# Streaming encoder layer on Trainium2: the last phase in blocks of 768, 768 and 576 tokens, with the sample in the last block and seven-product pairs in all three

## The chip, the cores and the metric

One NeuronCore of a Trainium2 chip runs the whole layer. The metric is device microseconds of one execution: the median of three runs before the change is 2979.64 us (2978.55 to 2980.76). TensorE is called PE in the profile (its weight loads PEld), VectorE DVE, ScalarE ACT, GpSimd POOL, SyncE SP.

## The reference

One encoder layer works on a prompt of 2048 tokens and on a sample of 64 tokens with caches of its own. Both have model width 1024; the FFN has 2816 columns. In short, for each of the two:

```
h = rms_norm(x) * (1 + sc1) + sh1
z = h @ w_in                      # conv pair, q, k, v, two gates
conv_out = conv_module(...)       # depthwise conv, layer norm, swish, projection
attn_out = band_attend(...) @ w_attn_out
merged = sigmoid(g_conv) * conv_out + sigmoid(g_attn) * attn_out
x = x + gt1 * (merged @ w_o)
h2 = rms_norm(x) * (1 + sc2) + sh2
gate, up = split(h2 @ w_ffn_in)
x = x + gt2 * ((silu(gate) * up) @ w_ffn_out)
```

The shifts, scales and gates (`sh`, `sc`, `gt`) differ between prompt and sample. All is float32.

## The kernel before

**Products.** TensorE multiplies float32 as a sum of two shorter numbers, high and low. Each product is three matmuls, high by high, high by low and low by high (`mm3`). Both operands must first be split: ScalarE copies the high half, VectorE or GpSimd subtracts it from the whole and writes the low half. For weights these are the tiles `whi` and `wlo`. For the 64 sample tokens the high and low halves lie side by side in 128 columns, so that two matmuls do (`mm2`); the two halves of the result are added later.

**Phases.** Up to about 1199 us the projections, the convolution, the attention and the gates run, in four blocks of tokens (`PBLOCKS`), and leave their results in DRAM. From there on the last phase runs (the loop over `CBLOCKS`, line 1823). It takes blocks of tokens, (0, 576), (576, 1344), (1344, 2112), where tokens 0 to 63 are the sample. The change touches this phase only. A block goes through these steps:

- *Merge* (`merge`, line 1690): in two chunks of tokens, the attention projection and the gating of the two branches. The gates come in by DMA a channel tile at a time (`gate_columns`), the branches' values by `load_mixed`. The chunks of the block of 576 are 320 and 256 tokens, those of a block of 768 are 384 and 384.
- *Output projection* (`wo`, line 1857): for each tile of 128 tokens, 1024 columns in two banks `pw`. The first `shared` of the eight steps of the sum are taken for all tiles of the chunk together, the others tile by tile.
- *Residual* (`residual`, line 1729, a generator for each tile): gate, add `x`, norm, transposes by TensorE (`pw<-ident,xn`), scale and shift, and the operands of the first FFN product, `b11`, `b21`, `b22` and the sums `t1` to `t4`, which are sums over the four quarters of the transposed block (first and second half of the tokens by first and second half of the 1024 columns). VectorE and ScalarE make them, 512 elements at a time.
- *Early half products* (line 2216 on): the first FFN product of a row goes by seven products instead of eight. Those with `b11` and `b21` need only the first half of the tokens, and for the first `EARLY` = 5 rows they are taken while the operands of the second half are still being made. Their results wait in `early`.
- *FFN rows*: 22 rows `f` of 128 gate and 128 up columns. `up` (line 1961) takes the products of a row, each 12 matmuls of `half` columns (288 or 384), with VectorE and ScalarE adding between them; `hidden` and `rest` write the result of a row, split, into `hid`.
- *Second FFN product*, for a pair of rows at a time, between the products of the next rows. The direct way (`down`, `add_down`) takes 12 matmuls of 512 columns for a tile and row pair (8 for the sample), and VectorE adds each tile's two halves into `acc`. The other way (`down_pair`, line 2053) takes seven products instead of eight for a pair of rows, two halves of the tokens and two halves of the columns. It needs sums of `hid` (tile `sums`, made in `rest`) and sums of weights, which GpSimd makes in `sum_second`, and each product is added by VectorE on its own. `seven(s, f)` (line 564) says which rows of which block go by it: rows 4 to 19 of the second and third block, none of the first.
- *End of a block*: the last two rows (four in the first block) are added, scaled and written out. In the last block GpSimd scales `acc` and adds `x1` ahead of the last matmuls (`scale`, `add_last`).

**Weights.** The class `Weights` (line 264) loads slabs in the order of `weight_order`, splits them ahead of their use (`split`, line 451) and keeps the split ones in a small ring. Sums of first-product weights (`s1` to `s4`) are made by GpSimd in the first block and stored to DRAM (`sum_d`), from where the later blocks read them. In `split` the low half of a slab goes to GpSimd as a rule; for `up` and `fo` slabs it goes to VectorE where GpSimd, by the planner's count, is more than 3000 ns behind TensorE:

```
late = key[0] in ("up", "fo") and self.stream.load["pool"] - self.stream.load["pe"] > POOL_BEHIND
e, name = (self.dve, "dve") if on_dve or late else (self.gps, "pool")
```

**Order.** The program is written as generators with due times (`stream`, `turns`, `work`), which keep a running count of what each engine has been given. A scheduler then puts the instructions of each engine in a fixed order, and each engine works through its own in that order. Every operation passes through one helper, so that the profile shows line 102 for nearly all of them; they are told apart by the names of their tiles (`pw` output projection, `ps` merge and first FFN product, `pd` second FFN product).

## Time and profile before

| what | us |
|---|---|
| median of the runs (lowest, highest) | 2979.64 (2978.55, 2980.76) |
| the profiled execution, its span | 2979.5, 2977.7 |
| first block of the last phase, from the first merge matmul to the last scaled sum | 1199.2 to 1715.2 |
| second block | 1715.2 to 2343.7 |
| third block, up to its last matmuls | 2343.7 to 2971.0 |
| last additions and the output | 2971.0 to 2977.7 |

The profile is of one execution. A line of the timeline gives start, length, engine, source line, operation, output and input tiles, shape, count, and in square brackets the idle time of the engine before it and what released it. In a group of instructions the columns are the shape and count, then busy time and the mean of one in ns, then the idle time before them. The chain of waits is followed back from the last instruction: at each step to what released it, or to the instruction before it on its engine. The mean granted clock of TensorE is 0.995 of full speed.

### The profile page before, as it was taken

What the parts mean: (1) busy time and instruction counts of PE and PEld (TensorE: products, weight loads), DVE (VectorE), ACT (ScalarE), POOL (GpSimd) and SP (SyncE); (2) the same over time, 40 slices, a digit from 0 to 9 for tenths busy, and PEclk for the clock granted to TensorE, in tenths of its full rate; (3) what the DMA queues carried; (4) which work ended last, traced back from release to release, by engine and by line L of the source; (5) the groups of instructions that cost most, each with busy time, mean ns of one, the idle gap of its engine ahead of it and who ended that gap; (6) DMA issues with size and microseconds to landing.
All of it is one profiled execution on the core that took longest, in us unless ns stands there. A gap on an engine that the chain in (4) does not pass through costs nothing.

```text
span 2977.7 us, 44838 instructions
## 1 busy us (share of the span) xinstructions
PE 2900.2 (97%) x16199; PEld 2593.1 (87%) x16199; DVE 2025.9 (68%) x3637; ACT 1356.8 (46%) x2441; POOL 1127.7 (38%) x727
## 2 busy tenths in 40 slices
PE   7999899999999999989999999999999999999999
PEld 4899777787888888888999999999999999999998
DVE  5797677767856886577777755666666557466666
ACT  2345642662456257464444345534444345344442
POOL 0201310111011102454466443255666741465667
PEclk9999999999999999999999999999999999999999
DMA  8889889878987798885444786333333975333333
GB/s 290 300 286 310 270 279 312 284 251 274 306 283 224 267 263 278 262 288 175 145 145 159 244 263 235 116 95 106 114 113 113 316 239 184 93 95 114 114 103 128
DMA packets 467723, 628.05 MB, mean 211 GB/s; under 512 B 36276, under 2 KB 314664, under 8 KB 467501
## 3 DMA queue, kind: packets, MB, share of 16 engines
q1 hardware_dynamic: 453456, 605.58, 62.8%
q10 hardware_dynamic: 14045, 19.60, 1.9%
q8 instruction: 127, 2.08, 0.3%
q14 instruction: 95, 0.78, 0.1%
HBM read 476.53 MB, written 148.54 MB: 210 GB/s over the span
## 4 chain that ended last, share of the span: by engine, by line
PE 82%; DVE 7%; DMA 4%; ACT 2%; issue 2%; POOL 2%; SPq 0%; ACTq 0%; POOLq 0%; DVEq 0%
PE ps L102 53%; PE pd L102 16%; PE pw L102 6%; DVE y L102 2%; PE sc L102 2%; PE po L102 2%; PE ptp L102 2%; DVE wlo L102 1%; PE pt L102 1%; DMA kk<-k_d 1%; ACT whi L102 1%; PE pa L102 1%; POOL r L102 1%; DVE pw L102 1%; DMA wst<-in_w_in 0%
## 5 line engine op out<-in xcount | busy, mean ns | idle before, releaser
L102 PE MATMUL ps<-t,whi 128*128 128x384 f32 (+1 forms) x2112 | 503.1, 322 | 8.7 <-ACT t L102 4.9
L102 POOL TENSOR_TENSOR wlo<-wst,whi 128x1024 fp32r<-128x1024 f32 (+1 forms) x156 | 356.4, 2294 | 279.0 <-ACT whi L102 262.6
L102 ACT ACTIVATE whi<-wst 128x1024 fp32r<-128x1024 f32 (+1 forms) x263 | 256.8, 979 | 331.2 <-PE ps L102 119.8
L102 PE MATMUL ps<-b,whi 128*128 128x384 f32 (+1 forms) x1584 | 381.7, 326 | 7.0 <-DVE early L102 3.6
L102 PEld LDWEIGHTS ps<-t,whi 128*128 128x128 f32 x2112 | 367.8, 188 | 16.3 <-ACT t L102 5.1
L102 DVE SCALAR_TENSOR_TENSOR y<-u,wd,y 128x512 f32<-128x512 f32 (+1 forms) x480 | 369.0, 773 | 6.3
L102 PE MATMUL ps<-hh,whi 128*128 128x512 f32 (+2 forms) x992 | 361.7, 365 | 0.0
L102 DVE TENSOR_TENSOR acc<-acc,pd 128x512 f32<-128x512 f32 x464 | 311.7, 685 | 62.7 <-PE pd L102 60.2
L102 PE MATMUL ps<-hl,whi 128*128 128x512 f32 (+2 forms) x992 | 345.6, 348 | 0.0
L102 PE MATMUL ps<-hh,wlo 128*128 128x512 f32 (+2 forms) x992 | 345.4, 348 | 0.0
L102 PE MATMUL ps<-t,wlo 128*128 128x384 f32 (+1 forms) x1056 | 339.4, 322 | 0.8 <-POOL wlo L102 0.7
L102 PE MATMUL pd<-whi,hid 128*128 128x512 f32 x972 | 314.8, 390 | 0.0
L102 PEld LDWEIGHTS ps<-b,whi 128*128 128x128 f32 x1584 | 278.7, 189 | 13.1 <-DVE early L102 4.5
L102 POOL TENSOR_TENSOR r<-t,mhalf 128x1 f32<-128x1 f32 (+3 forms) x68 | 83.6, 1232 | 462.1 <-DVE t L102 457.0
L102 PE MATMUL ps<-b,wlo 128*128 128x384 f32 (+1 forms) x792 | 257.3, 325 | 0.0
L102 ACT ACTIVATE pr<-pr,sm 128x640 f32<-128x640 f32 (+3 forms) x272 | 200.1, 747 | 112.1 <-DVE sm L102 109.5
L102 PEld LDWEIGHTS pd<-whi,hid 128*128 128x128 f32 x972 | 182.5, 188 | 37.7 <-ACT hid L102 0.7
L102 PEld LDWEIGHTS ps<-hh,wlo 128*128 128x128 f32 x992 | 186.7, 188 | 21.6
L102 PEld LDWEIGHTS ps<-hh,whi 128*128 128x128 f32 x992 | 187.2, 189 | 18.5 <-issue 1.6
L102 PEld LDWEIGHTS ps<-hl,whi 128*128 128x128 f32 x992 | 187.5, 189 | 15.5 <-issue 1.4
L102 PEld LDWEIGHTS ps<-t,wlo 128*128 128x128 f32 x1056 | 198.2, 188 | 2.2 <-POOL wlo L102 1.3
L102 PE MATMUL pd<-wlo,hid 128*128 128x512 f32 x508 | 198.6, 391 | 0.0
(226 smaller groups left out, 6170.6 us busy)
## 6 DMA issues: line engine op xcount, KB each, us to landing
whi<-w_din_h SPq DMA_DIRECT2D x72, 512.0 KB, 6.5
wlo<-w_din_l SPq DMA_DIRECT2D x72, 512.0 KB, 8.4
wst<-sum_d SPq DMA_DIRECT2D x132, 256.0 KB, 2.7
wfo<-in_w_ffn_out SPq DMA_DIRECT2D x64, 512.0 KB, 3.2
wmod<-in_w_ada SPq DMA_DIRECT2D x46, 512.0 KB, 6.5
sum_d<-ws SPq DMA_DIRECT2D x88, 256.0 KB, 2.8
wst<-in_w_ffn_in SPq DMA_DIRECT2D x84, 256.0 KB, 3.1
wst<-in_w_in SPq DMA_DIRECT2D x40, 512.0 KB, 8.8
```

What stands on the lines that cost most here:

```text
L102: self.last = f(*args, **kw)
```

## The change

The blocks of the last phase become the tokens (64, 832), (832, 1600) and (1600, 2112), and the sample (tokens 0 to 63) joins the last one (`MIXED` = 2). It lies in the middle there: two prompt tiles, the sample, two prompt tiles, so that each half of the tokens is 256 prompt tokens and 32 of the sample. The merges of that block have chunks of 320 (256 and the sample) and 256 tokens. In code:

- `block_tiles`, `block_chunks` and `width` take the place of `tile_chunks`; a chunk is a list of parts, so that `gate_columns` and `load_mixed` issue one DMA for each part.
- `seven`: in the first block the pairs f // 2 = 2, 4, 6, 8 go by seven products, in the two others all rows from 2 to 19.
- In the last block `down_pair` has two tiles in each product (`wide` = 256) and takes the sample directly with `mm2`, for which the last weight slab of a pair holds `b12` beside `b22` (`down_operands`). `hid` keeps the sample's high and low halves behind the prompt tokens (`both`), written by `hidden_sample`.
- In `rest` the split of the sum kept in `sums[2]` moves from the even row of a pair to the odd one, and the tile `sums` is taken only there.
- `scale` and `add_last` treat the sample's tile in the last block: its two halves are added with a ScalarE copy between two VectorE additions.
- `shared` is 6 of 8 steps wherever a chunk has two tiles.

```diff
...
 PBLOCKS = [(0, 576), (576, 1088), (1088, 1600), (1600, 2112)]
-CBLOCKS = [(0, 576), (576, 1344), (1344, 2112)]
+CBLOCKS = [(64, 832), (832, 1600), (1600, 2112)]
+MIXED = 2
 STEP_NS = 500.0
...
-def tile_chunks(lo, hi):
-    tiles = token_tiles(lo, hi)
-    t, n = tiles[(len(tiles) + 1) // 2 - 1]
-    return [(lo, t + n), (t + n, hi)]
+def block_tiles(s):
+    tiles = [(t, P, t - CBLOCKS[s][0]) for t in range(*CBLOCKS[s], P)]
+    if s == MIXED:
+        tiles = tiles[:2] + [(0, SMP, 2 * P)] + [(t, n, a + SMP) for t, n, a in tiles[2:]]
+    return tiles
+def block_chunks(s):
+    lo, hi = CBLOCKS[s]
+    n = (hi - lo) // 2
+    return [[(0, lo, n)] + [(n, 0, SMP)] * (s == MIXED), [(0, lo + n, n)]]
+def width(parts):
+    return sum(n for _, _, n in parts)
...
-        return {"b11": (0,), "t1": (0,), "t3": (0, 1)}.get(op, (1,))
+        return {"b11": (0,), "b12": (0,), "t1": (0,), "t3": (0, 1)}.get(op, (1,))
...
-    return s > 0 and 4 <= f < NF - 2
+    return 2 <= f < NF - 2 if s else f // 2 in (2, 4, 6, 8)
...
-DOWN_OPERANDS = (("b11", "b21"), ("t3", "t2"), ("t1", "t4"), ("b22",))
+def down_operands(s):
+    return ("b11", "b21"), ("t3", "t2"), ("t1", "t4"), ("b22", "b12") if s == MIXED else ("b22",)
...
                 if f >= 2 and seven(s, f - 2):
-                    yield from (("dn", s, f - 2, *DOWN_OPERANDS[i]) for i in {0: (0,), 2: (1, 2), 4: (3,)}.get(j, ()))
+                    yield from (("dn", s, f - 2, *down_operands(s)[i]) for i in {0: (0,), 2: (1, 2), 4: (3,)}.get(j, ()))
                 elif j == 0 and f >= 2 and f - 2 not in last_rows(s):
...
-            shared = KT - 2 if not s and c1 == hi else 4
+            shared = KT - 2 if len(grp) < 3 else 4
...
+        side = half - 2 * P if s == MIXED else 0
+        wide = half - side
+        inner = [slice(0, wide), slice(side, half)]
+        rows_at = [slice(i * wide, (i + 1) * wide) for i in range(2)]
+        both = slice(2 * wide, 2 * wide + 2 * SMP)
+        at_rows = {t: slice(a - (a > half) * (half - wide + side), a - (a > half) * (half - wide + side) + n) for t, n, a in tiles}
         def hidden(f, i, ps):
             h = hid_of(f)
-            c = slice(i * half, (i + 1) * half)
             stream.after("act", "dve")
-            if s:
-                split(h[:, 0, c], h[:, 1, c], ps)
+            split(h[:, 0, rows_at[i]], h[:, 1, rows_at[i]], ps[:, inner[i]])
+            hidden_sample(f, i, ps)
+        def hidden_sample(f, i, ps):
+            if s != MIXED:
                 return
-            hi = h[:, 0, SMP:][:, c]
-            act.activation(hi, ps, AF.Copy)
-            stream.after("dve", "act")
-            cut = 0 if i else SMP
-            if cut:
-                dve.tensor_tensor(h[:, 0, :cut], ps[:, :cut], hi[:, :cut].bitcast(F32), ALU.subtract)
-            dve.tensor_tensor(h[:, 1, c][:, cut:], ps[:, cut:], hi[:, cut:].bitcast(F32), ALU.subtract)
+            c = slice(0, side) if i else slice(wide, half)
+            hi, lo = (hid_of(f)[:, 0, both.start + l * SMP + i * side :][:, :side] for l in range(2))
+            stream.after("act", "dve")
+            split(hi, lo, ps[:, c])
...
                 return
-            if "t" not in sums:
-                sums["t"] = wk.tile([P, 4, 2, CW // 2], F32R, tag="m1", name="sums")
-            at = lambda i: [sums["t"][:, i, l, :half] for l in range(2)]
+            at = lambda i: [sums["t"][:, i, l, :wide] for l in range(2)]
+            z, whole, y = z[:, inner[0]], y, y[:, inner[1]]
             if f % 2 == 0:
+                hidden_sample(f, 1, whole)
                 sums["a21"], sums["s3"] = (
-                    wk.tile([P, CW // 2], F32, tag=name, name=name, bufs=1)[:, :half] for name in ("a21", "s3")
+                    wk.tile([P, CW // 2], F32, tag=name, name=name, bufs=1)[:, :wide] for name in ("a21", "s3")
                 )
...
                 stream.after("act", "dve")
-                split(*at(2), y)
                 act.activation(sums["s3"], y, AF.Copy)
                 return
-            hidden(f, 1, y)
-            t = bank("gp")
+            if "t" not in sums:
+                sums["t"] = wk.tile([P, 4, 2, CW // 2], F32R, tag="m1", name="sums")
+            hidden(f, 1, whole)
+            split(*at(2), sums["s3"])
+            t = bank("gp")[:, :wide]
             dve.tensor_tensor(t, y, sums["a21"], ALU.add)
...
-            a11, a12, a22 = (
-                [hid[0][:, e, l, i * half : (i + 1) * half] for l in range(2)] for e, i in ((0, 0), (1, 0), (1, 1))
-            )
-            s1, s2, s3, s4 = ([sums["t"][:, i, l, :half] for l in range(2)] for i in range(4))
-            n = len(tiles) // 2
+            a11, a12, a22 = ([hid[0][:, e, l, rows_at[i]] for l in range(2)] for e, i in ((0, 0), (1, 0), (1, 1)))
+            s1, s2, s3, s4 = ([sums["t"][:, i, l, :wide] for l in range(2)] for i in range(4))
+            n = wide // P
             zs = [bank_of("gp", "pd")]
...
                     stream.after("dve", "pe")
-                    dst = acc[p + i * n][:, 512 * e : 512 * e + 512]
+                    dst = acc[p + i * (len(tiles) - n)][:, 512 * e : 512 * e + 512]
                     dve.tensor_tensor(dst, dst, pss[p], ALU.add)
-            w = W.get(("dn", s, f, *DOWN_OPERANDS[0]))
+            def sample(ps, w, es, j):
+                for e, (h, l) in zip(es, ((t[0][:, i], t[1][:, i]) for t, i in w)):
+                    mm2(ps, hid[0][:, e, 0, both], h, l, e == es[0], e == es[1])
+                stream.after("dve", "pe")
+                dst = acc[n][:, 512 * j : 512 * j + 512]
+                dve.tensor_tensor(dst, dst, ps, ALU.add)
+            ops = down_operands(s)
+            w = W.get(("dn", s, f, *ops[0]))
             products(ys, a11, w, 0, True, False, 0, 0)
             yield
-            zs += [bank_of(tag, "pd") for tag in ("y1", "z1")]
+            zs += [bank_of(tag, "pd") for tag in ("y1", "z1")[: n - 1]]
             products(zs, a12, w, 1, True, True, 0, 0)
+            if s == MIXED:
+                sample(bank_of("gp", "pd"), ((w, 0), (w, 1)), (0, 1), 0)
             W.done()
-            w = W.get(("dn", s, f, *DOWN_OPERANDS[1]))
+            w = W.get(("dn", s, f, *ops[1]))
             products(zs, s3, w, 0, True, False, 1, 1)
...
             W.done()
-            w = W.get(("dn", s, f, *DOWN_OPERANDS[2]))
+            w = W.get(("dn", s, f, *ops[2]))
             products(ys, s1, w, 0, False, False, 1, 1)
...
             yield
-            w = W.get(("dn", s, f, *DOWN_OPERANDS[3]))
+            w = W.get(("dn", s, f, *ops[3]))
             products(ys, s4, w, 0, False, True, 0, 1)
+            if s == MIXED:
+                sample(bank_of("z1", "pd"), ((w, 0), (w, 1)), (1, 0), 1)
             W.done()
...
         def pieces():
-            return [(i, t, n, j) for i, (t, n) in enumerate(tiles) for j in range(2)]
+            return [(i, t, n, j) for i, (t, n, _) in enumerate(tiles) for j in range(2)]
...
-            gt = [wk.tile([P, 512], F32, tag="ws", name="gt", bufs=4) for _ in range(2)]
-            for j in range(2):
-                nc.sync.dma_start(gt[j], gt_d[1, 0:1, 512 * j : 512 * j + 512].to_broadcast([P, 512]))
-            ends["gt"] = gt
+            gt = ends["gt"] = {}
+            for which in {int(t < SMP) for t, _, _ in tiles}:
+                gt[which] = [wk.tile([P, 512], F32, tag="ws", name="gt", bufs=4) for _ in range(2)]
+                for j in range(2):
+                    nc.sync.dma_start(
+                        gt[which][j], gt_d[1, which : which + 1, 512 * j : 512 * j + 512].to_broadcast([P, 512])
+                    )
             yield stream.load["pe"] + DMA_LAG
             for k, (i, t, n, j) in enumerate(pieces()):
-                dst = acc[i][:n, 512 * j : 512 * j + 512]
-                gps.tensor_tensor(dst, dst, gt[j][:n], ALU.mult)
+                dst = acc[i][:, 512 * j : 512 * j + 512]
+                gps.tensor_tensor(dst, dst, gt[int(t < SMP)][j], ALU.mult)
                 ends["scaled"] = k
...
             for k, (i, t, n, j) in enumerate(pieces()):
-                ps = bank_of("gp", "pd")[:n]
-                c, f = slice(t - lo, t - lo + n), slice(512 * j, 512 * j + 512)
+                ps = bank_of("gp", "pd")
+                c, f = at_rows[t], slice(512 * j, 512 * j + 512)
                 for e, w in zip(last, ws):
                     h = hid_of(e)
-                    mm3(ps, h[:, 0, c], h[:, 1, c], w[0][:, 0, f], w[1][:, 0, f], e == last[0], e == last[-1])
+                    at = w[0][:, 0, f], w[1][:, 0, f], e == last[0], e == last[-1]
+                    if t < SMP:
+                        mm2(ps, h[:, 0, both], *at)
+                    else:
+                        mm3(ps, h[:, 0, c], h[:, 1, c], *at)
                 while ends.get("scaled" if after(k) else "added", -1) < k:
...
                 stream.after("dve", "pe")
-                dve.tensor_tensor(ps, ps, ends["gt"][j][:n], ALU.mult)
+                dve.tensor_tensor(ps, ps, ends["gt"][int(t < SMP)][j], ALU.mult)
                 dst = acc[i][:n, f]
+                if t < SMP:
+                    dve.tensor_tensor(ps, ps, acc[i][:, f], ALU.add)
+                    stream.after("act", "dve")
+                    act.activation(dst, ps[SMP : 2 * SMP], AF.Copy)
+                    stream.after("dve", "act")
+                    ps = ps[:n]
                 dve.tensor_tensor(dst, dst, ps, ALU.add)
...
```

## What the change does to the time: a prediction

> **What bounds the kernel now.** I read the page first, the busy times of each stage next, and then the chain of waits, the waits of TensorE and the timelines of the stages that the change touches.
>
> ```profile
> span 2977.7 us, 44838 instructions
> PE 2900.2 (97%) x16199; PEld 2593.1 (87%) x16199; DVE 2025.9 (68%) x3637; ACT 1356.8 (46%) x2441; POOL 1127.7 (38%) x727
> ```
>
> The profiled execution took 2979.5 us (span 2977.7), the runs have a median of 2979.64, so a sum made against the profiled one needs no correction beyond 0.1 us. TensorE is busy 97% of the span: work taken from it counts in full, and all else counts only where it makes TensorE wait. The stretches of the three blocks, the end, one stretch of direct rows in the block of 576 and one of pairs with seven products in a block of 768 follow; the columns are the stretch, its length, and busy us (instructions) of PE, PEld, DVE, ACT and POOL, then clock, DMA share, GB/s.
>
> ```profile
> 1199.20:1715.15 515.95, 501.55 (x3113) 461.56 (x3114) 364.89 (x622) 230.65 (x441) 268.32 (x169) 0.99 0.63 204
> 1715.15:2343.65 628.50, 627.16 (x3290) 584.27 (x3289) 388.96 (x645) 279.35 (x458) 348.44 (x203) 1.00 0.47 151
> 2343.65:2971.00 627.35, 625.92 (x3283) 583.02 (x3283) 386.36 (x642) 273.98 (x453) 345.20 (x205) 1.00 0.45 147
> ...
> 1484.00:1660.00 176.00, 175.22 (x1119) 162.85 (x1118) 126.99 (x195) 72.80 (x150) 116.98 (x75) 1.00 0.46 149
> 2000.00:2306.00 306.00, 306.00 (x1613) 287.51 (x1612) 198.78 (x328) 137.66 (x238) 200.58 (x122) 1.00 0.36 113
> ```
>
> The two blocks of 768 leave TensorE idle for 1.3 and 1.4 us each, the block of 576 for 14.4. So there are two places to gain: TensorE's work, and the gaps of the first block. Where the gaps lie, TensorE's waits from the last output-projection tile on say (us in all, times, longest): first the first block, then the second.
>
> ```profile
> PE ps L102 <- ACT t L102: 4.9, 1, 4.9
> PE ps L102 <- DVE early L102: 2.6, 1, 2.6
> PE ps L102 <- DVE u L102: 1.6, 1, 1.6
> PE ps L102 <- ACT early L102: 0.8, 2, 0.5
> ```
>
> ```profile
> PE ps L102 <- DVE early L102: 0.5, 1, 0.5
> PE ps L102 <- POOL wlo L102: 0.3, 1, 0.3
> PE ps L102 <- ACT early L102: 0.2, 1, 0.2
> ```
>
> That is 9.9 us against 1.0. The timeline of TensorE shows a second cost behind the long waits.
>
> ```profile
> 1306.69 0.39 PE L102 MATMUL pw<-whi,m 128*128 128x512 f32 x1
> ...
> 1318.72 0.73 PE L102 MATMUL ps<-b,whi 128*128 128x288 f32 x2 [2.63 <-DVE early L102]
> ...
> 1319.49 0.68 PE L102 MATMUL ps<-b,whi 128*128 128x288 f32 x2
> ...
> 1320.21 0.68 PE L102 MATMUL ps<-b,whi 128*128 128x288 f32 x2
> ...
> 1322.85 0.42 PE L102 MATMUL ps<-b,whi 128*128 128x288 f32 x2
> ...
> 1323.25 0.43 PE L102 MATMUL ps<-b,whi 128*128 128x288 f32 x2
> ...
> 1329.06 0.58 PE L102 MATMUL ps<-t,whi 128*128 128x288 f32 x1 [4.85 <-ACT t L102]
> ```
>
> A triplet of 288-wide matmuls takes 0.40 us (1322.85 to 1323.25), behind the wait 0.72 (1319.49 to 1320.21). Four triplets go so, 4 x 0.32 = 1.3 us, and the same follows the 4.85 us wait. The start of the first block thus costs 9.9 + 2 x 1.3 = 12.5 us, that of a block of 768 only 1.0.
>
> **1. Fewer matmuls.** The durations come from the chain of waits, one pair of rows of the 768 block and one of the 576 block (start, us, what).
>
> ```profile
> 2634.21 20.93 PE ps L102 x120
> ...
> 2665.58 6.16 PE pd L102 x27
> ...
> 1483.53 11.20 PE ps L102 x83
> 1494.73 12.71 PE pd L102 x56
> ```
>
> A `pd` matmul costs 6.16/27 = 0.228 us (12.71/56 = 0.227), a 384-wide one 20.93/120 = 0.174, a 288-wide one 11.20/83 = 0.135. The first FFN product keeps its matmuls, only the order of the three half widths becomes 384, 384, 288. The second loses some. A direct pair of rows takes 72 `pd` matmuls with 768 tokens, 56 with 576 (48 for four tiles, 8 for the sample); by seven products 63, and in the mixed last block 42 + 8 = 50.
>
> Before: 11 x 56 + 2 x (8 x 63 + 3 x 72) = 616 + 1440 = 2056. After: (4 x 63 + 7 x 72) + (9 x 63 + 2 x 72) + (9 x 50 + 2 x 56) = 756 + 711 + 562 = 2029. The order in which the instructions stand on TensorE has these 27 fewer too. 27 x 0.2276 = 6.1 us, in stages where TensorE is 99.6 to 100% busy: **-6.1**, sure.
>
> **2. Start of the first block.** It now has 3 + 3 tiles and 384 columns, so the ten half products of the five early rows (120 matmuls) cover 120 x 0.174 = 20.9 us in place of 120 x 0.135 = 16.2. These 4.7 us are about the wait for `t` (4.85): it goes with its 1.3 us of slow clock, and the 1.6 us for `u` behind it is worked off: -7.8. What stays is the wait for `early`: the operand sums of the early rows are still made by GpSimd here, and ScalarE and VectorE stand in order behind them.
>
> ```profile
> 1316.24 1.15 ACT L102 ACTIVATE whi<-ws 128x512 fp32r<-128x512 f32 x2 [2.32 <-POOL ws L102]
> ...
> 1316.90 1.08 DVE L102 TENSOR_TENSOR wlo<-ws,whi 128x512 fp32r<-128x512 f32 x1 [5.17 <-ACT whi L102]
> ```
>
> Bounds: it becomes like the second block's start, 1.0 - 12.5 = -11.5; or the third tile's work on VectorE uses up nearly all cover, -2. I take **-8**.
>
> **3. Start of the last block.** This is the reverse: 3 + 2 tiles (the sample the third) with 288 columns, where a 768 block stood. In its instruction order TensorE reaches the first product with `t3` after 72 half-product matmuls and 16 transposes, 72 x 0.135 + 16 x 0.13 = 11.8 us behind the last output-projection matmul (0.13 by the eight of 1.03 us below). `t3` needs the last tile's norm, transposes and sums. In the second block these took from 1850.90 to 1874.9, 24.0 us with three tiles:
>
> ```profile
> 1850.90 0.39 PE L102 MATMUL pw<-whi,m 128*128 128x512 f32 x1
> ...
> 1853.26 1.03 PE L102 MATMUL pw<-ident,xn 128*128 128x128 f32 x8
> ...
> 1874.24 0.68 DVE L102 TENSOR_TENSOR t<-pw,t 128x512 fp32r<-128x512 f32 x1
> ```
>
> One tile less is about nine 512-wide VectorE steps of 0.6 each (the last row, net of its overlap with the next), 5.4 us, so `t3` is there after 18.6: a wait of 6.8, then 1.3 of slow clock, about 1 more for the rows behind: **+9**. Queued behind the waiting matmul are the rest of the half products, though their data are there. Bounds: +4 if the order lets the cover decide (4.7 less cover, next to the 1.0 there), +12 if it goes as the first block did (12.5). The merges before it are 320 and 256 wide rather than 384 and need 16 + 4 + 2 more DMA issues on SP for the sample's gates, inputs and scales; SP only queues loads that have a whole merge of lead: +0.5 (0 to +3).
>
> **4. Pairs of the last block.** The rule that moves a slab's low half from GpSimd to VectorE fires far oftener there: by the order of the instructions 63 `up` slabs of 1024 in the last block against 15 before. Each pair now has on VectorE 7 slabs of 1024, 16 accumulations of 512, 14 operations of 288, 11 of 256, 4 of 32; GpSimd keeps 12 of 512. TensorE's pair takes 168 x 0.135 + 50 x 0.228 = 34.1 us.
>
> ```profile
> L102 DVE TENSOR_TENSOR acc<-acc,pd 128x512 f32<-128x512 f32 x50 | 33.0, 682 | 15.2 <-PE pd L102 15.1
> ...
> L102 DVE TENSOR_TENSOR wlo<-wfo,whi 128x1024 fp32r<-128x1024 f32 x5 | 8.8, 1767 | 2.4 <-ACT whi L102 2.4
> ...
> L102 DVE SCALAR_TENSOR_TENSOR s<-tg,ps 128x288 f32<-128x288 f32 x10 | 4.5, 449 | 3.0 <-ACT tg L102 3.0
> ...
> L102 DVE TENSOR_TENSOR hid<-ps,hid 128x64 fp32r<-128x64 f32 x10 | 2.2, 217 | 2.4 <-ACT hid L102 2.4
> ```
>
> ```profile
> 1869.92 1.22 DVE L102 TENSOR_TENSOR wlo<-wst,whi 128x1024 fp32r<-128x1024 f32 x1
> 1871.05 0.41 DVE L102 TENSOR_SCALAR pw<-pw,A,B 128x128 f32<-128x128 f32 x1
> ```
>
> Each operation overlaps the next by about 0.08 (1.22 against 1871.05 - 1869.92 = 1.13). Net of that: 16 x 0.60 + 7 x 1.14 + 14 x 0.37 + 11 x 0.33 + 4 x 0.14 = 9.6 + 8.0 + 5.2 + 3.6 + 0.6 = 27.0 us of 34.1, 79%; with 1767 ns a slab, as beside a busy GpSimd, 27.0 + 7 x 0.63 = 31.4, 92%. At 127/176 = 72% TensorE lost only 0.8 of 176 us. So VectorE is not full, but more of its in-order work stands ahead of the `hid` that TensorE needs. Cover: one row of first products. I take **+2** (0 to +14: two such slabs a pair, 1.26 us, in eleven pairs).
>
> **5. The rest.** Each of the four pairs by seven products in the first block adds nine accumulations on VectorE (21 for 12, 9 x 0.6 = 5.4 us) and the sums and splits of `hid`, beside GpSimd's operand sums; in the 768 blocks the same pairs cost TensorE nothing (306.00 busy of 306.00), and a direct pair stands between any two here: +1 (0 to +4). The split of a pair's second sum moves to its odd row, off the path. In the end the sample's piece waits for a ScalarE copy between VectorE additions; 66 matmuls hide it, except for the last pieces:
>
> ```profile
> 2955.83 15.18 PE pd L102 x66
> ...
> 2973.63 0.69 DVE L102 TENSOR_TENSOR acc<-acc,pd 128x512 f32<-128x512 f32 x1
> ```
>
> The last pieces belong to prompt tiles again: +0.3 (0 to +4).
>
> **Sum:** -6.1 - 8 + 9 + 0.5 + 2 + 1 + 0.3 = -1.3, so 2979.5 - 1.3 = 2978.
>
> **Rivals.** *A faster start, both times.* Block 0 starts like the second block (-11.5), the last block's start costs only its cover (+4), pairs cost nothing: -6.1 - 11.5 + 4 + 0.5 + 1 + 0.3 = -11.8, 2968. For it: the 1.0 us of the second block's start; against it: `t3` stands early in TensorE's order, and GpSimd's sums stay in block 0.
>
> *VectorE decides in the last block.* It begins when a slab takes 1.77 us rather than 1.14 and two of them a pair stand just ahead of a `hid` split: 11 x 1.26 = 13.9 in place of 2, -1.3 + 11.9 = +10.6, 2990. For it: 63 slabs instead of 15, the two rows below, and 72% being the highest load seen without loss; against it: GpSimd is busy there only 12 x 1.3 = 15.6 of 34.1 us, 46%, where the 1767 ns were measured at 117/176 = 66%.
>
> ```profile
> 1560.02 1.92 DVE L102 TENSOR_TENSOR wlo<-wst,whi 128x512 fp32r<-128x512 f32 x1 [0.16 <-ACT whi L102]
> ...
> 1567.63 0.69 DVE L102 TENSOR_TENSOR wlo<-ws,whi 128x512 fp32r<-128x512 f32 x1
> ```
>
> The same operation takes 1.92 us or 0.69. The Trainium skill, "SBUF — State Buffer", section "Who interferes with whom", says that a VectorE instruction with two SBUF inputs and a GpSimd instruction that reads SBUF exclude each other for a whole instruction; these rows agree with it, and it speaks against moving slabs to VectorE. By that rule alone each of the seven slabs could lose up to 1.23 us, 8.6 in a pair, which would fill VectorE (35.6 of 34.1).
>
> *It does not do what it says.* The counts on TensorE rule it out.
>
> **Numbers.** Forecast 0.42, own range 2970 to 2986 by the bounds of steps 2 to 4; faster rival 0.28; VectorE rival 0.30. About 0.2%, 6 us, is what a measurement of this kernel can tell from no change. Of the forecast 0.13 lies more than 6 us below, 0.22 within, 0.07 above; of the first rival 0.27 below; of the second 0.28 above, the rest within. So faster 0.40, same 0.25, slower 0.35. The range reaches past both rivals' values, 2964 to 2993.
>
> **What would show it.** 27 fewer `pd` matmuls at 0.228. Step 2: TensorE's waits from the first block's last output-projection matmul on fall from 9.9 to some 4. Step 3: one wait of some 7 us for `t` or `pw` at the last block's start. Step 4: TensorE's idle time in the last block's pairs stays under 0.3 us a pair; more, released by `hid` or `wlo` of VectorE, is the second rival. The forecast is wrong if a pair of the last block takes over 35 us, or if steps 2 and 3 differ from each other by more than 5.

## The result

The changed kernel takes 3001.14 us (median of four runs, 2996.57 to 3004.87) where the kernel before takes 2979.10 in the same session: a ratio of 1.0073, 95% interval 1.0055 to 1.0090. It is some 22 us slower. Forecast were 2978 and a range of 2964 to 2993.

The page of the changed kernel (the helper's line is now 115; span, and busy time of each engine):

```profile
span 2998.3 us, 45004 instructions
PE 2903.1 (97%) x16172; PEld 2584.4 (86%) x16172; DVE 2136.0 (71%) x3786; ACT 1389.4 (46%) x2560; POOL 1093.1 (36%) x728
```

TensorE has 27 recorded matmuls fewer and yet 2.9 us more busy time; VectorE has 110 us more. To see where the 20.6 us of span lie, the last phase is cut into three stretches for each block: the merges and output projection, the start (from the last output-projection matmul to the first `pd` matmul), and the FFN rows. Busy times of the kernel before, first, second and third block, in that order (columns as in the prediction):

```profile
1199.23:1306.69 107.46, 107.01 (x631) 97.00 (x632) 61.46 (x130) 54.21 (x89) 52.59 (x26) 0.98 0.86 272
1306.69:1358.52 51.83, 41.83 (x282) 39.71 (x281) 43.40 (x79) 31.12 (x62) 24.02 (x19) 0.93 0.82 287
1358.52:1714.99 356.47, 352.55 (x2202) 324.70 (x2201) 260.03 (x415) 145.31 (x291) 191.56 (x124) 1.00 0.53 172
1714.99:1850.90 135.91, 135.91 (x704) 124.48 (x703) 69.53 (x121) 59.60 (x87) 56.84 (x28) 1.00 0.73 238
1850.90:1900.83 49.93, 48.97 (x282) 47.85 (x281) 44.80 (x74) 30.84 (x55) 8.76 (x4) 1.00 0.53 183
1900.83:2343.48 442.65, 442.27 (x2305) 411.93 (x2305) 274.46 (x450) 188.74 (x318) 282.84 (x171) 1.00 0.38 121
2343.48:2479.73 136.25, 136.16 (x704) 124.41 (x703) 68.20 (x122) 57.95 (x86) 56.79 (x30) 1.00 0.78 261
2479.73:2529.70 49.97, 48.99 (x283) 47.88 (x281) 44.80 (x74) 30.84 (x55) 8.77 (x4) 1.00 0.53 182
2529.70:2972.35 442.65, 442.29 (x2305) 411.67 (x2304) 274.86 (x451) 185.35 (x314) 279.81 (x171) 1.00 0.34 108
```

The same of the changed kernel:

```profile
1196.81:1332.88 136.07, 136.07 (x704) 124.56 (x704) 67.84 (x119) 58.91 (x89) 50.80 (x26) 1.00 0.75 246
1332.88:1394.52 61.64, 53.10 (x282) 50.12 (x281) 54.99 (x87) 34.59 (x68) 31.31 (x24) 0.94 0.70 239
1394.52:1852.62 458.10, 453.15 (x2341) 417.47 (x2341) 319.55 (x481) 176.73 (x336) 221.36 (x155) 1.00 0.44 142
1852.62:1988.59 135.97, 135.97 (x704) 124.48 (x703) 68.39 (x121) 58.70 (x87) 56.87 (x28) 1.00 0.66 214
1988.59:2038.58 49.99, 49.00 (x283) 47.83 (x282) 44.82 (x74) 30.87 (x55) 12.93 (x7) 1.00 0.53 186
2038.58:2479.80 441.22, 440.71 (x2297) 410.05 (x2296) 285.88 (x466) 193.06 (x329) 291.11 (x178) 1.00 0.38 118
2479.80:2590.18 110.38, 105.91 (x633) 95.24 (x631) 64.22 (x131) 51.27 (x83) 56.35 (x28) 1.00 0.91 292
2590.18:2640.52 50.34, 40.77 (x283) 39.54 (x282) 37.95 (x67) 28.72 (x53) 9.67 (x7) 0.90 0.53 185
2640.52:2992.91 352.39, 346.76 (x2148) 313.49 (x2146) 305.70 (x519) 183.57 (x376) 197.00 (x129) 1.00 0.42 132
```

| stretch | before, sum | after, sum | difference |
|---|---|---|---|
| up to the last phase | 1199.2 | 1196.8 | -2.4 |
| three merges and projections | 379.6 | 382.4 | +2.8 |
| three starts | 151.7 | 162.0 | +10.2 |
| three stretches of rows | 1241.8 | 1251.7 | +9.9 |

The first line is not the change's: the phase before the blocks ended between 1190.9 and 1199.9 us in all the profiles here, the two above and those of the experiments. The starts make a table of two by two. A wide start (768 tokens) takes 50.0 us in a later block and 61.6 in the first; a narrow one (576) takes 51.8 in the first and 50.3 in the last, though it has less to multiply (40.8 to 41.8 us of TensorE). The kernel before put the narrow block first and paid one long start; the changed one pays two. In the rows, 6.1 us of matmuls went, and yet they take 9.9 us more in all.

### The profile page after: what moved, and what is told of

It is laid out like the page before. It is cut to its first block, busy times and chain, and to the rows that moved or that the text cites. A ratio compares the mean times of both kernels' runs of the same rounds, so it can differ in the third digit from the quotient of the medians.

```text
span 2998.3 us, 45004 instructions
## 1 busy us (share of the span) xinstructions
PE 2903.1 (97%) x16172; PEld 2584.4 (86%) x16172; DVE 2136.0 (71%) x3786; ACT 1389.4 (46%) x2560; POOL 1093.1 (36%) x728
## 3 DMA queue, kind: packets, MB, share of 16 engines
q1 hardware_dynamic: 458016, 605.58, 62.6%
## 4 chain that ended last, share of the span: by engine, by line
PE 74%; DVE 13%; DMA 5%; ACT 3%; issue 3%; POOL 1%; SPq 0%; ACTq 0%; DVEq 0%; POOLq 0%
PE ps L115 49%; PE pd L115 12%; PE pw L115 6%; DVE wlo L115 3%; DVE y L115 3%; PE sc L115 2%; PE po L115 2%; PE ptp L115 2%; DVE acc L115 1%; DVE ps L115 1%; PE pt L115 1%; ACT whi L115 1%; PE pa L115 1%; POOL r L115 1%; DVE sums L115 1%
## 5 line engine op out<-in xcount | busy, mean ns | idle before, releaser
L115 ACT ACTIVATE whi<-wst 128x1024 fp32r<-128x1024 f32 (+1 forms) x273 | 265.9, 980 | 297.6 <-PE ps L115 115.9
L115 PEld LDWEIGHTS ps<-t,whi 128*128 128x128 f32 x2112 | 369.5, 189 | 29.4 <-ACT t L115 10.2
L115 DVE TENSOR_TENSOR acc<-acc,pd 128x512 f32<-128x512 f32 x487 | 318.7, 682 | 38.6 <-PE pd L115 37.0
L115 POOL TENSOR_TENSOR wlo<-wst,whi 128x1024 fp32r<-128x1024 f32 (+1 forms) x114 | 256.3, 2260 | 221.1 <-ACT whi L115 200.9
L115 PE MATMUL pd<-whi,hid 128*128 128x512 f32 x882 | 288.8, 391 | 0.3 <-DVE acc L115 0.3
L115 DVE TENSOR_TENSOR wlo<-wst,whi 128x1024 fp32r<-128x1024 f32 (+1 forms) x159 | 216.1, 1360 | 91.3 <-ACT whi L115 90.6
L115 POOL TENSOR_TENSOR wlo<-wfo,whi 128x512 fp32r<-128x512 f32 (+1 forms) x91 | 145.9, 1619 | 146.3 <-ACT whi L115 146.3
```

Of the source, the lines that this page charges most:

```text
L115: self.last = f(*args, **kw)
```

## The experiments

Each is the changed kernel with one edit, unless it says otherwise; each ratio is to the kernel before on the same chip, where the changed kernel has 1.0073 (1.0055 to 1.0090).

**1. The order at the start.**

```diff
-                product(ps, ops.use(e, op), b, first, last)
+                with tc.issue_after(pe.last.ins) if not e and op in ("s3", "s2") else nullcontext():
+                    product(ps, ops.use(e, op), b, first, last)
```

> The changed kernel, with the first products of the first row (t3, t2) held behind the last early half product on TensorE, in all blocks; only the last block's order moves. My theory: the 8.3 us wait for t in the last block's start is one of place, since 48 half products (48 x 0.135 = 6.5 us) stand behind the waiting matmul; the wait falls to about 2, its slow clock shrinks, and the time falls by 6 to 8 us, to about 2993. Rival: the chain of the last tile (norm, transposes, sums on VectorE) needs all of that time whatever TensorE does meanwhile and the half products' results load VectorE ahead of it, so the wait only moves: within 2 us of 3000.

The ratio is 1.0071 (1.0054 to 1.0088). The last start takes 49.7 us, no less than where nothing of it is edited (47.7 to 51.2 us in the changed kernel and the versions of experiments 6, 9 and 10). The timeline of TensorE: in the changed kernel the wait stands before `t`, here before the half product of row 3, equally long.

```profile
2612.16 0.61 PE L115 MATMUL ps<-t,whi 128*128 128x288 f32 x1 [8.29 <-ACT t L115]
```

```profile
2614.26 0.82 PE L115 MATMUL ps<-b,whi 128*128 128x288 f32 x2 [8.32 <-ACT t L115]
```

The rival was right: place in TensorE's order was not it. By the program, the half product of row 3 goes to a bank that the output projection's last tiles hold; experiment 5 tries that.

**2. GpSimd keeps the slabs in the last block.**

```diff
-            late = ... > POOL_BEHIND
+            late = ... > POOL_BEHIND and not self.calm
...
+        W.calm = s == MIXED
```

> The changed kernel, with the rule that sends slabs to VectorE switched off in the last block: the 67 low halves go back to GpSimd, 7 a pair. My theory: VectorE's load (32 of 35 us in a pair) is what costs 1.2 us a pair; without it a pair takes 33.9 us, the time falls by 8 to 10 us, to about 2991, with GpSimd at 15.5 + 7 x 2.4 = 32 of 34 us. Rival: the weights of a pair are too much for its 34 us whoever splits them; GpSimd falls behind, TensorE waits for wlo of GpSimd, and the time is the same or longer, 3000 to 3020.

The ratio is 1.0042 (1.0027 to 1.0057), 9.2 us less by the ratios. Three pairs of the last block in the changed kernel, then here:

```profile
2789.65:2895.07 105.42, 103.96 (x656) 94.33 (x655) 96.25 (x157) 57.06 (x118) 56.53 (x37) 1.00 0.43 135
```

```profile
2788.22:2889.52 101.30, 101.30 (x655) 94.13 (x654) 65.40 (x136) 56.93 (x117) 95.83 (x58) 1.00 0.45 141
```

A pair goes from 35.1 to 33.8 us, VectorE from 91% to 65% busy, GpSimd from 54% to 95%, and TensorE never idles in these pairs. All rows of the block take 342.8 in place of 352.4 us. The theory held. Nothing waits for GpSimd at 95% in these pairs; in the whole block TensorE waits for its `wlo` twice, 2.8 us. From the first to the last `pd` matmul the block takes 342.4 to 343.6 us in the three versions with no slab on VectorE there (2, 8 and 11). In the changed kernel and the five others with 63 slabs on VectorE between these two matmuls (1, 6, 9, 10 and 12) it takes 347.4 to 352.2. The slabs thus cost 4 to 10 us, and 9.6 is near the upper end; why 10 and 12 lie lowest was not followed up. Operations of VectorE in those pairs of the changed kernel (group, count, then busy us and mean ns):

```profile
L115 DVE TENSOR_TENSOR wlo<-wst,whi 128x1024 fp32r<-128x1024 f32 x19 | 31.9, 1678 | 0.3 <-ACT whi L115 0.3
...
L115 DVE TENSOR_TENSOR sums<-s,sums 128x256 fp32r<-128x256 f32 x3 | 4.2, 1391 | 0.0
...
L115 DVE TENSOR_TENSOR sums<-ps,sums 128x256 fp32r<-128x256 f32 x9 | 3.7, 420 | 0.0
```

A slab takes 1678 ns here, not the 1226 that five such slabs took in the last block of the kernel before (2628 to 2935 us), and seven of them a pair are 11.7 us.

**3. The last block all direct.**

```diff
-    return 2 <= f < NF - 2 if s else f // 2 in (2, 4, 6, 8)
+    return s == 1 and 2 <= f < NF - 2 or s == 0 and f // 2 in (2, 4, 6, 8)
```

> The changed kernel, with all pairs of the last block direct: 54 pd matmuls more, 54 x 0.228 = 12.3 us. My theory: the pairs by seven products in the last block cost about 10 us of stalls beside what they save, so this gains back most: 3000 + 12.3 - 10 = 3002, TensorE idle under 0.2 us a pair. Rival: the stalls belong to the narrow block and stay with direct pairs: 3010 to 3012.

The ratio is 1.0071 (1.0056 to 1.0086). The last block's rows:

```profile
2636.73:2989.63 352.90, 352.17 (x2202) 324.48 (x2200) 193.78 (x355) 144.75 (x267) 182.33 (x86) 1.00 0.41 129
```

352.9 us with 54 matmuls (12.3 us) more: nine pairs by seven products had saved 0.5 us there, as the theory had it. With experiment 2 beside it, the same pairs save 10.1 us (342.8 against 352.9) once GpSimd keeps the slabs: not the narrow block as such, but the slabs on VectorE ate up the gain.

**4. The narrow block first again, with the changed code.**

```diff
-CBLOCKS = [(64, 832), (832, 1600), (1600, 2112)]
-MIXED = 2
+CBLOCKS = [(64, 576), (576, 1344), (1344, 2112)]
+MIXED = 0
...
-    return 2 <= f < NF - 2 if s else f // 2 in (2, 4, 6, 8)
+    return s > 0 and 2 <= f < NF - 2
```

> The changed code with blocks of 576, 768, 768 again, the sample in the middle of the first, pairs by seven products from row 2 on in the two others and none in the first. My theory: the slow start costs some 12 us for a first block (operand sums made by GpSimd) and some 12 us for a narrow block, and before the change one block paid both at once; so here it is paid once: 2979 less 1.4 us for the one pair more in each 768 block, 2976. Rival: the sample in the middle, with its two more small splits a row, is what costs: over 2985.

The ratio is 1.0018 (1.0008 to 1.0027). The first block's merges, and the three starts:

```profile
1194.16:1308.27 114.11, 107.66 (x632) 96.90 (x633) 65.64 (x130) 54.77 (x89) 53.81 (x27) 0.99 0.83 260
1308.27:1360.91 52.64, 42.00 (x282) 39.69 (x281) 43.06 (x76) 30.64 (x65) 25.14 (x20) 0.94 0.78 270
1855.06:1905.00 49.94, 48.96 (x282) 47.83 (x281) 45.14 (x74) 30.51 (x54) 13.44 (x7) 1.00 0.52 181
2483.60:2533.53 49.93, 48.97 (x282) 47.86 (x281) 45.13 (x74) 30.50 (x54) 13.48 (x7) 1.00 0.52 181
```

The starts are as expected, one long one. The total is not: the merges of the first block take 6.7 us more than before (114.1 against 107.5). The sample's chunk now has two DMAs for the gates of each piece, and VectorE's longest wait for one is 5.6 us there (3.7 before); but all its waits for them come to 8.3 us against 9.5, so the trace does not make them the cause, and it stays open. The rival's cause, the small splits in the rows, is not it either: the rows of the first block take 357.4 us against 356.5. What is true of the rival is that the changed layout costs some us, in the merges.

**5. Free banks for the early half products.**

```diff
-            pss = [[row_bank(i, j) for j in range(2)] for i in range(len(grp))]
+            pss = [[row_bank(i + (len(grp) < 3), j) for j in range(2)] for i in range(len(grp))]
```

> The changed kernel, with the output projection of a chunk of two tiles in four banks of the pool gp, so that the banks y1 and z1 are free for the half products of the early rows 3 and 4. Held behind t in the earlier run, the wait of 8.3 us did not go but moved to the half product of row 3. My theory now: it waits there for the bank that the last chunk's first tile holds until its sums are made, so the 48 half products of rows 3 and 4 are no cover; with free banks they are 48 x 0.135 = 6.5 us of cover, the wait falls to about 2 and the last block's start from 50.3 to 43 us: the time 6 to 8 us less than the changed kernel. Rival: the half products wait for the last tile's data or for VectorE's and ScalarE's reading of the earlier ones, whatever the bank: within 2 us of the changed kernel.

The ratio is 1.0069 (1.0052 to 1.0086), some 1 us less than the changed kernel by the ratios, where the theory had 6 to 8. TensorE's waits from the last output-projection matmul on:

```profile
PE ps L115 <- DVE t L115: 3.2, 2, 1.7
PE ps L115 <- ACT t L115: 2.1, 1, 2.1
PE ps L115 <- DMA wlo<-w_dfi_l: 0.6, 1, 0.6
```

The wait of 8.3 us is gone, but 5.3 us of other waits for `t` follow: VectorE and ScalarE make one operand after another. The first `pd` matmul comes earlier in this order, so the start is taken up to the end of the first pair's `pd` matmuls: 59.9 us instead of 63.1. Some 3 us were the banks'; the rest is the operands' own chain.

**6. The first block's operand sums later.**

```diff
-        W.hold = False
-        W.presum()
...
         for step, f in ((first, 3), (second, 2), (first, 4), (second, 3), (second, 4)):
             step(f)
             W.fill()
+        W.hold = False
+        W.presum()
```

> The changed kernel, with the operand sums of the first block's weights (GpSimd) and their splits held back until the ten half products are given out. My theory: the first block's start (61.7 us, 12 more than that of the second block) is long because the sums' splits stand on ScalarE and VectorE, in order, ahead of the last tile's operands; then the waits for early and t (about 8 us) shrink by half, and some of it comes back as a wait for the first operand sums: 2 to 6 us less than the changed kernel. Rival: the sums are needed so early that the wait only changes its name: within 2 us, or longer.

The ratio is 1.0074 (1.0058 to 1.0090), and the first start takes 63.6 us. The rival was right: the waits for `t` and `early` stay (6.4 us, 6.5 in the changed kernel), and that for VectorE's `u` grows from 1.6 to 3.4 us.

**7. The kernel before, with two edits.** The edit of 5, and in the blocks of 768:

```diff
-    return s > 0 and 4 <= f < NF - 2
+    return s > 0 and 2 <= f < NF - 2
```

with the split of the second sum moved as in the change.

> The kernel before, with two edits: pairs by seven products from row 2 on in its two blocks of 768 (the split of one sum moved to the odd row, as in the change), and the four gp banks for a chunk of two tiles. My theory: 18 matmuls of 0.228 fewer, less one wait of 0.5 us in each block, -2.8 us, and a shorter start of the first block, -4 to -6: 2970 against 2977 to 2979. Rival: the first block's start is held by the operand sums as well, so the banks alone give nothing there: 2975 to 2976.

2976.74 us against 2979.31: 0.9990 (0.9981 to 1.0000). It is the fastest version here, but the interval reaches to no change, and the result lies by the rival's 2975 to 2976 and not by the theory's 2970. Its first start and the three stretches of rows:

```profile
1302.89:1353.41 50.52, 42.53 (x283) 39.93 (x282) 44.32 (x78) 30.72 (x62) 24.56 (x19) 0.93 0.81 288
1353.41:1710.26 356.85, 352.75 (x2203) 324.69 (x2202) 259.09 (x416) 145.57 (x291) 191.43 (x124) 1.00 0.52 171
1896.83:2338.05 441.22, 440.71 (x2297) 410.02 (x2296) 285.28 (x468) 193.23 (x329) 291.12 (x178) 1.00 0.37 121
2525.07:2966.27 441.20, 440.71 (x2296) 409.81 (x2295) 285.55 (x468) 189.83 (x325) 287.55 (x178) 1.00 0.34 108
```

The pair more in each wide block brings 1.4 us twice. The start with the banks is 1.3 us shorter, no more than unedited starts differ among themselves (61.2 to 62.6 us in the first block of the versions that leave it alone).

**8. Edits 2 and 5 together.**

> The changed kernel with both cures of the last block: GpSimd keeps the slabs' low halves there, and free banks for rows 3 and 4. If the two causes are separate the gains add: 9 + 7 us less than the changed kernel, about 1.0020 of the kernel before. Rival: with GpSimd at 32 of 34 us and more of TensorE's work done early, the first rows' slabs come late from GpSimd, and only one of the two gains is left, about 1.0042.

The ratio is 1.0029 (1.0018 to 1.0040): the last start takes 46.3 us and the rows behind it 344.0. The banks add 1.1 us to experiment 2's gain by the profiles (48.7 + 342.8 there) and 4 by the ratios, whose intervals overlap; the theory's 7 is not reached.

**9. The first block all direct.**

```diff
-    return 2 <= f < NF - 2 if s else f // 2 in (2, 4, 6, 8)
+    return s > 0 and 2 <= f < NF - 2
```

> The changed kernel, with all pairs of the first block direct: 36 pd matmuls more, 8.2 us. My theory: in the first block, where GpSimd makes the operand sums as well, a pair by seven products with the direct pair behind it takes 92.2 us for 89.3 us of matmuls, 2.9 us of waits (for VectorE's accumulations) against the 2.05 us that it saves; so the four pairs lose more than they save: 8.2 - 11.5, some 3 us less than the changed kernel, and pairs of 42.0 us (168 x 0.174 + 72 x 0.228 = 45.6) without waits. Rival: the waits belong to the first block's operand sums and stay: 6 to 8 us more than the changed kernel.

The ratio is 1.0075 (1.0060 to 1.0090). (The 42.0 in the expectation is a slip; the sum beside it is meant.) The first fence has the first block's rows here, the second a pair by seven products and the direct one behind it in the changed kernel, the third two direct pairs here:

```profile
1394.77:1852.20 457.43, 456.84 (x2377) 425.22 (x2377) 240.96 (x362) 159.43 (x292) 254.69 (x174) 1.00 0.42 142
```

```profile
1629.76:1721.93 92.17, 90.70 (x472) 83.76 (x471) 65.61 (x98) 36.44 (x72) 49.77 (x35) 1.00 0.36 114
```

```profile
1629.95:1675.67 45.72, 45.72 (x242) 42.87 (x240) 22.72 (x34) 16.07 (x31) 29.05 (x20) 1.00 0.35 115
1675.67:1721.39 45.72, 45.72 (x242) 42.87 (x240) 22.75 (x34) 16.08 (x31) 28.93 (x20) 1.00 0.34 116
```

92.17 against 91.44 us: in the first block a pair by seven products is slower than a direct one by 0.7, though it has nine matmuls fewer. The waits go with it: in these rows they come to 4.6 us in the changed kernel, 2.9 of them for VectorE's `acc`, and to 0.6 here. So 36 matmuls more cost nothing (457.4 against 458.1). From the first to the last `pd` matmul the block takes 457.2 us in both versions with direct pairs (9 and 11) and 457.8 to 457.9 in the nine others with the four pairs, so that the sign is sure. The theory had it right, and the rival is excluded; the total is too coarse to show the gain, which is 0.7 us and not 3.

**10. GpSimd keeps the slabs in the first block's start.** As edit 2, but on for the first block until its rows begin.

> The changed kernel, with the rule that sends slabs to VectorE switched off in the first block until its FFN rows begin: about nine low halves of 512 go from VectorE to GpSimd in the first block's start. My theory: that start is long (61.7 us for 49.9 in the second block) because VectorE has 12 us more work there than in the second block's start; with nine times 0.69 us moved off it the start is 4 to 6 us shorter. Rival: GpSimd, which makes the sums themselves, is what the chain waits for; with more work on it the start gets longer, 62 to 66 us.

The ratio is 1.0067 (1.0050 to 1.0083), and the start takes 60.6 us, with VectorE at 48.6 instead of 55.0 us busy. Neither theory holds: with 6 us less of VectorE's work the start is 1.1 us shorter, and versions that leave it alone take 61.2 to 62.6. The waits for `t` are gone, and those for `early` have grown from 3.2 to 7.8 us.

**11. Edits 2, 5 and 9 together.**

> The changed kernel with three cures: first block direct, GpSimd keeps the slabs in the last block, free banks for rows 3 and 4. If the gains add: 3 + 9 + 2.5 us less than the changed kernel, 1.0023 of the kernel before; the rest, two starts of 12 us in place of one, stays. Rival: the cures together reach the kernel before, so that the two starts cost nothing: 0.998 to 1.000.

The ratio is 1.0035 (1.0024 to 1.0046), no less than without edit 9: the first theory, without its 3 us for the first block. In the profile the rows now come to 0.4 us less than in the kernel before. What stays are the starts, 4.3 us more in sum (61.2 us in the first block and 44.9 in the last), and the merges, 5.1 us more.

**12. No stored splits.** The five early rows' split weights are not stored, so every block splits them anew.

```diff
-KEPT = ("qkv", "in", "fi")
+KEPT = ("qkv", "in")
```

> The changed kernel, in which the split weights of the five early rows are not stored to DRAM in the first block; the two later blocks load and split the raw weights again. It is read by its starts (last output-projection matmul to first pd matmul: 61.7, 50.0, 50.3 us in the changed kernel), not by its total. In the chain of waits of the first block's start ScalarE waits 3 us for a raw weight whose DMA takes 6.7 us behind stores on SP's queue. My theory: these stores, with the operand sums', make the first start long; without them it falls to 52 to 56 us, and the second block's start grows little, to 50 to 53. Rival: the splitting itself on ScalarE and VectorE is the cause; then the first start stays at 60 to 62, and the second and third grow by some 5 to 10 us. Second rival: GpSimd's operand sums are the cause, which only the first block makes: 60 to 62 in the first, 50 to 52 in the second.

The ratio is 1.0089 (1.0063 to 1.0115). The first start and the second:

```profile
1335.53:1397.52 61.99, 52.19 (x282) 49.15 (x281) 55.65 (x87) 34.81 (x68) 31.07 (x24) 0.97 0.54 173
1991.55:2048.33 56.78, 49.94 (x282) 47.67 (x281) 50.03 (x79) 34.16 (x61) 15.23 (x12) 1.00 0.40 130
```

The stores are not the cause: without them the first start is as long. But the second block, which now loads and splits raw weights too and makes no operand sums, takes 56.8 in place of 50.0 us. Of the 11.7 us that the first block's wide start takes more than the second's, 6.8 are matched by this. The third start does not grow, against what the rival said of it: it takes 48.3 us, within the 47.7 to 51.2 of the unedited ones. For the other 5 us of the first start the operand sums remain, which no run took away. ScalarE's waits for them in the first start of the changed kernel are these (us in all, times, longest); the second start has none:

```profile
ACT whi L115 <- POOL ws L115: 7.0, 3, 3.2
```

In experiment 6, which gave the sums out later, ScalarE still waits 8.6 us for them in the start.

## Why the prediction was wrong

- *Step 1, the matmuls (-6.1).* The recorded `pd` matmuls are 882 + 463 + 456 + 228 = 2029, and they are shorter work. But only the middle block turned them into time: its rows went from 442.65 to 441.22. The savings of the other two were used up by what steps 4 and 5 mis-sized.
- *Step 2, the first start (-8): the step that failed most.* The cost of this start was 12.5 before and is 61.6 - 50.0 + 1.0 = 12.6 after, so the term is +0.1. The step read "these 4.7 us are about the wait for `t`" as a matter of cover. More columns lengthen the cover, but the third tile brings its own VectorE and ScalarE work to the same chain. The 4.9 us for `t` fell to two waits of 1.4 and 1.9 and those for `early` and `u` stayed, so that TensorE's waits fell from 9.9 to 8.5 us, where some 4 were forecast. And TensorE took 53.1 us, at a clock of 0.94, for the matmuls that take it 49.0 in the second block: 4.1 us that go with the slow clock, where 2.6 had been counted before and half of it should have gone. The bound of -2 was nearest, and even that was too hopeful. What makes this start long is only in part known: loading and splitting raw weights matches 6.8 us of it, the operand sums are a candidate for the rest, and how much the third tile adds was not tried apart.
- *Step 3, the last start (+9, and +0.5 for the merges).* The start takes 50.3 us against the 39.3 that the first narrow start would have taken without its 12.5, a cost of 11.0; the start that stood there before cost 1.0, so the term is +10.0. The merges before it take 110.4 us against 107.5, +2.9 (110.4 to 113.8 in the eleven profiles with this layout). The size was right within its bounds. What was read wrongly is "their data are there": the half products behind the waiting matmul were held by a bank (experiments 1 and 5), and once it is free TensorE waits for the operands' chain instead, 5.3 us.
- *Step 4, the pairs of the last block (+2).* This term was undersized: 9.6 us by experiment 2. The second rival had the mechanism, VectorE with seven slabs of 1.68 us, and its price of 13.9 us was nearer than 2. A pair took 35.1 us, over the 35 that had been named as the sign of being wrong, and TensorE's idle time was 0.5 us a pair, over the 0.3; the recorded waits there were for ScalarE's `s` and VectorE's `acc` and not for `hid` or `wlo`. The estimate of 79% load took 1.14 us a slab; the upper one of 92% was close to the 91% measured. The mistake was to take the lower one, and with it next to no cost.
- *Step 5, the pairs of the first block (+1, at most +4).* Undersized as well: 36 matmuls worth 8.2 us went and 0.7 us came as a loss (experiment 9). The four pairs thus cost TensorE 8.9 us, twice the upper bound; 4 us of it are recorded waits, for `acc` above all. "A direct pair stands between any two" was no relief: the waits come all the same. The end (+0.3) did not change: from the last `pd` matmul to the end it takes 5.4 us both times.

Put together, the terms as measured are -6.1 + 0.1 + 10.0 + 2.9 + 9.6 + 8.9 = 25.4 us against the 22.9 us of the three stages in the table; the last two prices were read from experiments of their own, and the 2.5 us between are not assigned. In words: 27 matmuls fewer, two long starts in place of one, and in two of three blocks pairs that save nothing. The range missed because steps 2 and 5 came out beyond their bad ends and step 4 far above its middle. It was also narrower than the bounds that it named: the bad ends of steps 2 to 4 alone lie 6 + 3 + 12 = 21 us above the forecast, at 2999. The three steps were treated as separate luck, but they are alike: work of VectorE and ScalarE ahead of what TensorE waits for. For steps 4 and 5 experiments 2 and 9 show it; for step 2 it is an inference.

## What to carry to other kernels

Weight preparation costs the same for a narrow block as for a wide one, so a scheme that saves matmuls by adding VectorE work pays only where VectorE has room for both: here it saved 1.4 us for one pair more in a later wide block, and nothing in the narrow one or in the first. In the narrow one it was enough to leave the weights' low halves to GpSimd, and the same pairs saved 10.1 us. If one block must have a slow start for one reason, a second one can be nearly free in the same block, as it was here (a narrow first start takes 51.8 us, a narrow last one 50.3); look at which costs a layout lets coincide before moving them apart. And a wait that a trace names after one operand may be only the first of a chain: experiments 1, 5 and 10 took it away and found the next one behind it.

## What the runs showed that was not expected

The idle time that the trace gives for a wait is less than the wait costs. In the 92.17 us of experiment 9's second fence TensorE idles for 1.5, but 92.17 us are 2.9 more than its matmuls (336 x 0.174 + 135 x 0.228 = 89.2). The timeline of TensorE shows a part of it:

```profile
1666.53 0.34 PE L115 MATMUL ps<-t,wlo 128*128 128x384 f32 x1
1667.69 0.50 PE L115 MATMUL pd<-whi,sums 128*128 128x512 f32 x1 [0.82 <-DVE acc L115]
1668.03 0.39 PE L115 MATMUL pd<-wlo,sums 128*128 128x512 f32 x1
1668.26 0.63 PE L115 MATMUL pd<-whi,sums 128*128 128x512 f32 x2
```

The matmul behind the wait is followed after 0.34 us, the next after 0.23, which is 0.1 us more. Ahead of it, 1.16 us pass from 1666.53 to 1667.69, for a matmul of 0.17 and a recorded wait of 0.82: nearly 0.2 more. The stretch has two such waits, 0.82 and 0.57 us, so that this makes some 0.6 of the missing 1.4 us; the rest stands in gaps for which the trace records no wait.

The same split of 256 columns takes VectorE 1391 ns when both inputs lie in SBUF (`sums<-s,sums`, the one that the change moved to the odd row) and 420 ns when one is a matmul's result (`sums<-ps,sums`), with GpSimd busy 54% of the time. The Trainium skill, "SBUF — State Buffer", section "Who interferes with whom", says that it is VectorE's second SBUF input that collides with GpSimd's reads; these two rows agree with it. How busy GpSimd is does not give the price, though: in the last block of experiment 2, with GpSimd 95% busy in the pairs, the nine operations with both inputs in SBUF took from 418 to 2620 ns, half of them under 600, and those with a matmul's result never more than 425. The edit that was counted as off the path thus put 1 us a pair on the fullest engine of the changed kernel.
